# First modulation of a hybrid diffusion block: from split row products to raw fp32 weights as stationary operand

## The chip, the cores and the metric

One core of a Trainium2 chip. The metric is device time in microseconds of one execution; lower is better. The kernel is one layer of a diffusion backbone on 1024 latent tokens and 256 context tokens of width 1024, all in fp32.

## What is computed

The change touches the first few steps of the layer, the modulation vectors and the first RMSNorm:

```python
mod_l = (jax.nn.silu(c) @ w_mod[i] + b_mod[i])[:, None, :]
mod_c = jax.nn.silu(c_ctx) @ w_mod[i] + b_mod[i]
sh1, sc1, g1, sh2, sc2, g2 = jnp.split(mod_l, 6, axis=-1)
csh1, csc1, cg1, csh2, csc2, cg2 = jnp.split(mod_c, 6, axis=-1)
hl = modulate(rmsnorm(xl, norm1_w[i]), sh1, sc1)      # rmsnorm * (1 + scale) + shift
hc = modulate(rmsnorm(xc, norm1_w[i]), csh1, csc1)
...
xbc_l, dt_l, z_l, f_l, uv_l, gate_l = jnp.split(hl @ w_in, IN_SPLIT, axis=-1)
```

Everything after it (state space scan, Fourier mixing, gated MLPs, convolutional MLP, final norm) uses `hl` and `hc`, directly or through what is made of them.

## The kernel before

Tokens lie along the free dimension, channels on the partitions: `xT` holds the latent tokens as 8 tiles of 128 channels x 1024 tokens, `ctxT` the context. Large products run on TensorE in the reduced type fp32r, each operand split into a high and a low part (`split`, `wsplit`): ScalarE (ACT) copies the high part, VectorE (DVE) or GpSimd (POOL) subtracts to get the low part, and `mm3` adds three products, high x high, high x low and low x high. Small or delicate products run in plain fp32 with no split; the trace shows each of these as two TensorE records.

The start of the program, which the change touches, has these steps:

- **Squares (L194 to L204).** ACT squares the 8 tiles of `xT` as they land (L198, L201). DVE adds them into two accumulators `qx` (L202, six adds) and these into one (L203). `tok_sums` (L188) then sums over the partitions on TensorE: eight fp32 products with 128 columns of `qx` as stationary operand and one column of ones as moving operand, into `psx`.
- **Norm factor (`rstd_bcast`, L171).** DVE scales the sum (`rvx`, L173), POOL takes the power -0.5 (`rrx`, L175), DVE builds two diagonal tiles (`dgx`, L180), TensorE spreads them over the partitions with a matrix of ones (L183), ACT copies the result to `rbx`. The same for the context (`pssc`, `rrc`, `rbc`).
- **Modulation rows (`mod_rows(k)`, L234).** For each of 8 channel tiles k, two weight tiles `wm` (128 x 4 x 256) are split (ACT L239, POOL or DVE L240), and 16 products (L243) stream 256 weight columns past a 4-column stationary operand `csp`, the high and low parts of silu(c) and silu(c_ctx). The result is 4 rows of 256; DVE copies it to `mrow` (L246), and two fp32 products with the selector `sel` (L257) turn it into columns and add high and low.
- **Normalised tokens (L258 to L273).** DVE finishes `mods` (L258, L260), scales `xT` by it (L266), ACT adds the shift into the high part `hh` (L267), DVE makes the low part `hl` (L268); the same for the context (L271 to L273).
- **First products of the projection.** As tile k of `hh` and `hl` is there, TensorE adds its share to `psx` of weight tile `wx8` (L153, L155, L157), to the context's `psc`, and to the two halves of `psdl` (`dt_mm`, L356): per step k ten records with 512 columns and three with 256. When all 8 steps are in, the convolution on `psx` starts and the rest of the program follows.

The order of instructions on each engine is fixed when the program is built, by a scheduler that works on the dependencies; `tc.high_priority` moves a step ahead in it. Each engine then works strictly in its order. All transfers go out on SP's queue.

Of the kernel before, what the change touches and what calls it, by code (L numbers as in the profile page):

```python
# [8 lines left out]
F32 = mybir.dt.float32  # L9
F32R = mybir.dt.float32r  # L10
AF = mybir.ActivationFunctionType
ALU = mybir.AluOpType
AX = mybir.AxisListType

P = 128
D = 1024
KT = D // P
L = 1024
LC = 256
NH = 16  # L20
NCH = L // P
# [6 lines left out]
PRE, CRIT, CHAIN = 250, 200, 700  # L28
# [4 lines left out]
def hybrid_block_kernel(ctx: ExitStack, tc: tile.TileContext, a, dbg=None):  # L33
    nc = tc.nc
    V, S, G, PE, SY = nc.vector, nc.scalar, nc.gpsimd, nc.tensor, nc.sync

    def pool(name, bufs=1, **kw):
        return tc.alloc_tile_pool(name=name, bufs=bufs, **kw)

    const = pool("const")  # L40
# [11 lines left out]
    def ps_small(name, tag="c"):  # L52
        return pss.tile([P, 512], F32, tag=tag, name=name)
# [6 lines left out]
    def bc(ap, shape):  # L60
        return ap.broadcast_to(shape)
# [4 lines left out]
    s2 = pool("s2", bufs=2, side="right")  # L66
# [3 lines left out]
    ident, ones = cst[:, 0, :], cst[:, 1, :]  # L70
# [3 lines left out]
    wm0 = []  # L74
# [39 lines left out]
    sc_ = const.tile([P, KT, 2], F32, name="silc")  # L114
    S.activation(sc_, cvec, AF.Tanh, scale=0.5)
    V.scalar_tensor_tensor(sc_, sc_, 1.0, cvec, op0=ALU.add, op1=ALU.mult)
    V.tensor_scalar(sc_, sc_, 0.5, None, op0=ALU.mult)
    csp = const.tile([P, KT, 4], F32R, name="csp")
    S.activation(csp[:, :, 0:2], sc_, AF.Copy)
    V.tensor_tensor(csp[:, :, 2:4], sc_, csp.bitcast(F32)[:, :, 0:2], op=ALU.subtract)  # L120
    sel = const.tile([4, 2], F32, name="sel")
    V.tensor_tensor(sel, ident[0:4, 0:2], ident[0:4, 2:4], op=ALU.add)

    def late_consts():
        r = [load(sh, a[n], n) for sh, n in (([P, KT], "n2w"), ([P, KT], "nfw"), ([P, KT], "ssdd"), ([P, KT], "ssdn"),
                                             ([P, 44, 3], "fconvw"), ([P, 44], "fconvb"))]
        return r
# [31 lines left out]
    def f32(t):  # L159
        return t.bitcast(F32)  # L160
# [10 lines left out]
    def rstd_bcast(ss, n, dim, out, diag, tags, name, scale=1.0):  # L171
        v_ = const.tile([P, 16], F32, tag="rs_v", name="rv" + name, bufs=2)
        V.tensor_scalar(v_[:, 0:n], ss, scale / dim, EPS, op0=ALU.mult, op1=ALU.add)  # L173
        r_ = const.tile([P, 16], F32, tag="rs_r", name="rr" + name, bufs=2)
        G.tensor_tensor(r_[:, 0:n], v_[:, 0:n], expo[:, 0:n], op=ALU.pow)  # L175
        for i, tg in enumerate(tags):
            m = min(4, n - 4 * i)
            w_ = m * P
            dg = diag[:, 512 * i:512 * i + w_]
            V.tensor_tensor(dg.rearrange("p (n c) -> p n c", n=m), bc(ident.unsqueeze(1), [P, m, P]),  # L180
                            bc(r_[:, 4 * i:4 * i + m].unsqueeze(2), [P, m, P]), op=ALU.mult)
            ps = ps_small(f"rb{name}{i}", tg)
            last_op["PE"] = PE.matmul(ps[:, 0:w_], ones, dg, start=True, stop=True)  # L183
            if out is not None:
                S.activation(out[:, 512 * i:512 * i + w_], ps[:, 0:w_], AF.Copy)
        return ps[:, 0:w_]

    def tok_sums(ps, src, n, c0=0):  # L188
        for t in range(n):
            PE.matmul(ps[:, c0 + t:c0 + t + 1], src[:, t * P:(t + 1) * P], ones[:, 0:1], start=True, stop=True)  # L190


    psx = ps_small("psx", "c")
    qx = [tpool.tile([P, L], F32, tag=("tmp", "zz")[i], name=f"qx{i}", bufs=1) for i in range(2)]  # L194
    for k in range(KT):
        xk = xT[k // 4][:, k % 4, :]
        if k < 2:
            S.activation(qx[k], xk, AF.Square)  # L198
            continue
        q = s2.tile([P, L], F32, tag="CT", name=f"sqx{k}")  # L200
        S.activation(q, xk, AF.Square)  # L201
        V.tensor_tensor(qx[k % 2], qx[k % 2], q, op=ALU.add)  # L202
    V.tensor_tensor(qx[0], qx[0], qx[1], op=ALU.add)  # L203
    tok_sums(psx, qx[0], NCH)  # L204
    ssx = psx[:, 0:NCH]
    rbx = tpool.tile([P, L], F32, tag="tmp", name="rbx", bufs=1)
    dgx = tpool.tile([P, L], F32, tag="zz", name="dgx", bufs=1)
    with tc.high_priority(offset=CHAIN):
        rstd_bcast(ssx, NCH, float(D), rbx, dgx, ("y", "c2"), "x")

    hch = ctxp.tile([P, KT, LC], F32R, name="hch")
# [15 lines left out]
    rstd_bcast(ssc, 2, float(D), rbc, dgc, ("y",), "c")  # L227
    psmod = ps_small("psmod", "t")
    mods = const.tile([P, KT, 2, 2], F32, name="mods")
    crow = [p_[0:4, 256:512] for p_ in (psmod, ps_small("psrow", "c"))]  # L230
    mrt = s2.tile([4, 2, 256], F32, tag="CT", name="mrow")
    mrow = [mrt[:, i, :] for i in range(2)]

    def mod_rows(k):  # L234
        for i in range(2):
            wm = wm0[k][i]
            wh = s2.tile([P, 4, 256], F32R, tag="BT", name=f"wmh{k}{i}")
            wl = s2.tile([P, 4, 256], F32R, tag="Bt", name=f"wml{k}{i}")
            S.activation(wh, wm, AF.Copy)  # L239
            (G if i == 0 and k > 1 else V).tensor_tensor(wl, wm, f32(wh), op=ALU.subtract)  # L240
            for r in range(4):
                for q in range(2):
                    PE.matmul(crow[k % 2], csp[:, 4 * i + r, :], (wh, wl)[q][:, r, :], start=i + r + q == 0,  # L243
                              stop=i + r + q == 5)
        with tc.high_priority(offset=CHAIN):
            V.tensor_copy(mrow[k % 2], crow[k % 2])  # L246

    Hr = [dram.tile([P, L], F32, name=f"Hr{k}") for k in range(KT)]
    hh = [None] * KT
    hl = [None] * KT  # L250
    raws = []
    for k in range(KT):
        mod_rows(k)
        with tc.high_priority(offset=CHAIN):
            for s_ in range(2):
                o = 4 * k + 2 * s_
                PE.matmul(psmod[:, o:o + 2], mrow[k % 2][:, s_ * P:(s_ + 1) * P], sel, start=True, stop=True)  # L257
            V.tensor_tensor(mods[:, k], psmod[:, 4 * k:4 * k + 4].rearrange("p (s v) -> p s v", s=2),  # L258
                            bc(bmod[:, k:k + 9:8].unsqueeze(2), [P, 2, 2]), op=ALU.add)
            V.scalar_tensor_tensor(mods[:, k, 1], mods[:, k, 1], 1.0, bc(n1w[:, k:k + 1], [P, 2]),  # L260
                                   op0=ALU.add, op1=ALU.mult)
        shl, Al, shc, Ac = mods[:, k, 0, 0:1], mods[:, k, 1, 0:1], mods[:, k, 0, 1:2], mods[:, k, 1, 1:2]
        hh[k] = hpool.tile([P, L], F32R, tag="h", name=f"hh{k}")
        hl[k] = hpool.tile([P, L], F32R, tag="h", name=f"hl{k}")
        xk = xT[k // 4][:, k % 4, :]
        V.scalar_tensor_tensor(xk, xk, Al, rbx, op0=ALU.mult, op1=ALU.mult)  # L266
        last_op["hh"] = S.activation(hh[k], xk, AF.Identity, bias=shl)  # L267
        V.scalar_tensor_tensor(hl[k], xk, shl, f32(hh[k]), op0=ALU.add, op1=ALU.subtract)  # L268
        raws.append((k, xk, shl))
        ck = ctxT[k // 4][:, k % 4, :]  # L270
        V.scalar_tensor_tensor(ck, ck, Ac, rbc, op0=ALU.mult, op1=ALU.mult)  # L271
        S.activation(hch[:, k, :], ck, AF.Identity, bias=shc)
        last_op["h"] = V.scalar_tensor_tensor(hcl[:, k, :], ck, shc, f32(hch)[:, k, :],  # L273
                                              op0=ALU.add, op1=ALU.subtract)
# [317 lines left out]
    BT, Bt, CT = gi  # L592
# [115 lines left out]
    for g in range(4):  # L708
        psF = [ps_small(f"psF{g}{i}", ("c", "c2")[i]) for i in range(2)]
        for l_ in range(NCH):  # L710
            PE.matmul(psF[l_ // 4][:, (l_ % 4) * P:(l_ % 4 + 1) * P], fT[g][:, l_ * P:(l_ + 1) * P], tabc,
                      start=True, stop=True)
# [525 lines left out]
    def wpair(src, nm, raw=None):  # L1238
        if raw is None:
            raw = wx.tile([P, HB], F32, tag="rw", name=f"r{nm}", bufs=5)  # L1240
            SY.dma_start(raw.rearrange("p (k c) -> p k c", c=P), src)
        t = wpool.tile([P, 2, HB], F32R, tag="w", name=f"p{nm}")
        S.activation(t[:, 0, :], raw, AF.Copy)  # L1243
        G.tensor_tensor(t[:, 1, :], raw, f32(t)[:, 0, :], op=ALU.subtract)  # L1244
        v = t.rearrange("p q (k c) -> p q k c", c=P)
        return v[:, 0], v[:, 1]
# [23 lines left out]
    for d in PAIRS:  # L1270
        sg = tpool.tile([P, L], F32, tag="acc", name=f"sf{d}")
        SY.dma_start(sg, Sg[1][d])
        with tc.high_priority(offset=PRE):
# [5 lines left out]
            wh, wl = wpair(None, f"wfd{d}", we.rearrange("p a b c -> p (a b c)"))  # L1279
# [3 lines left out]
        for par, n in enumerate((NE, NO)):  # L1283
            o, q = [(pa[par][:, 0:n], slice(0, n))], [(pb[par][:, 0:n], slice(0, n))]
# [18 lines left out]
    for g in range(4):  # L1303
        t = tpool.tile([P, L], F32, tag=("tmp", "zz")[g % 2], name=f"gm{g}", bufs=1)
# [5 lines left out]
    for i, d in enumerate(PAIRS):  # L1310
# [9 lines left out]
        p_, th_, tl_ = (hpool, "h", "h") if d < 4 else (xp, "x", "x")  # L1320
# [186 lines left out]
    for ci, kc in enumerate(FF_CHUNKS[:-1]):  # L1507
# [3 lines left out]
        for i in range(0, len(seq), 2):  # L1511
            m = min(2, len(seq) - i)
            r = xp.tile([P, 2, HB], F32, tag="x", name=f"gr{ci}{i}")
            for q in range(m):
                p, k = seq[i + q]
                SY.dma_start(r[:, q, :], Gd[j0 // 2 + k][:, WHERE[p], :])
            p_, th_, tl_ = (xp, "x", "x") if i < 8 and ci < 3 else (hpool, "h", "h")
# [197 lines left out]
```

## Time and profile before

| | us |
|---|---|
| median of 3 runs (lowest, highest) | 1870.4 (1862.96, 1873.94) |
| the profiled execution, its own time | 1878.45 |
| its span in the profile | 1876.6 |
| TensorE (PE) busy in it | 1751.9 |
| VectorE (DVE) busy | 1347.3 |
| ScalarE (ACT) busy | 899.3 |
| GpSimd (POOL) busy | 808.3 |

The profiled execution lies 0.4% above the median; 1.85 us of it lie outside the span. All instants below are microseconds from the start of the span.

### The profile page before, as it was taken

What the parts mean: (1) busy time and instruction counts of PE and PEld (TensorE: products, weight loads), DVE (VectorE), ACT (ScalarE), POOL (GpSimd) and SP (SyncE); (2) the same over time, 40 slices, a digit from 0 to 9 for tenths busy, and PEclk for the clock granted to TensorE, in tenths of its full rate; (3) what the DMA queues carried; (4) which work ended last, traced back from release to release, by engine and by line L of the source; (5) the groups of instructions that cost most, each with busy time, mean ns of one, the idle gap of its engine ahead of it and who ended that gap; (6) DMA issues with size and microseconds to landing.
All of it is one profiled execution on the core that took longest, in us unless ns stands there. A gap on an engine that the chain in (4) does not pass through costs nothing. (4 is left out here: it accounts for less than half of the span.)

```text
span 1876.6 us, 23660 instructions
## 1 busy us (share of the span) xinstructions
PE 1751.9 (93%) x8172; PEld 1413.7 (75%) x8172; DVE 1347.3 (72%) x1855; ACT 899.3 (48%) x1605; POOL 808.3 (43%) x541
## 2 busy tenths in 40 slices
PE   4899998988999989999899999989999999899988
PEld 3688676776678868888688888868888888677767
DVE  6775668658873765558849535988878787977986
ACT  5544366665752344445434235545555455533433
POOL 3222254326531555444646745433333333554443
PEclk8899999999999989999998999999999999999998
DMA  9212374634563325665346364022332235653532
GB/s 337 90 60 67 102 202 139 188 111 143 156 227 123 123 74 196 230 223 181 118 141 207 129 230 135 29 90 102 117 108 96 96 108 172 231 168 107 169 91 90
DMA packets 147487, 267.70 MB, mean 143 GB/s; under 512 B 15772, under 2 KB 56604, under 8 KB 145960
## 3 DMA queue, kind: packets, MB, share of 16 engines
q1 hardware_dynamic: 147368, 266.20, 43.4%
q8 instruction: 64, 1.05, 0.2%
q14 instruction: 55, 0.45, 0.1%
HBM read 208.85 MB, written 57.29 MB: 142 GB/s over the span
## 5 line engine op out<-in xcount | busy, mean ns | idle before, releaser
L293 DVE SCALAR_TENSOR_TENSOR acc<-psx,convw,acc 128x1023 f32<-128x1023 f32 (+1 forms) x48 | 61.3, 1276 | 27.1 <-ACT acc L289 26.9
L568 DVE SCALAR_TENSOR_TENSOR rf<-rs,ncuml,rf 128x128 f32<-128x128 f32 x128 | 56.2, 487 | 29.5 <-ACT rf L567 21.2
L1244 POOL TENSOR_TENSOR pwo<-rwo,pwo 128x512 fp32r<-128x512 f32 x32 | 47.0, 1475 | 47.0 <-ACT pwo L1243 43.5
L861 POOL TENSOR_TENSOR w1up<-A11up,w1up 128x512 fp32r<-128x512 f32 x20 | 27.9, 1395 | 72.3 <-ACT w1up L860 72.3
L166 ACT ACTIVATE gh<-gr 128x1024 fp32r<-128x1024 f32 (+1 forms) x36 | 37.1, 1032 | 40.6 <-DMA gr<-Gd 37.8
L861 POOL TENSOR_TENSOR w7up<-S3up,w7up 128x512 fp32r<-128x512 f32 x18 | 23.7, 1317 | 74.5 <-ACT w7up L860 39.4
L567 ACT ACTIVATE rf<-rf,ncuml 128x128 f32<-128x128 f32 x128 | 40.8, 390 | 29.2 <-DMA rf<-Rd 27.1
L1531 DVE SCALAR_TENSOR_TENSOR xf<-Yd,g,xf 128x512 f32<-128x512 f32 x64 | 46.8, 742 | 10.0 <-PE Yd L871 10.0
L157 PE MATMUL pso<-mh,pwo 128*128 128x512 f32 x128 | 50.2, 392 | 0.0
L153 PE MATMUL pso<-mh,pwo 128*128 128x512 f32 x128 | 49.8, 390 | 0.0
L155 PE MATMUL pso<-ml,pwo 128*128 128x512 f32 x128 | 49.8, 389 | 0.0
L574 ACT ACTIVATE rs<-cbm,dtl 128x128 f32<-128x128 f32 x128 | 44.9, 390 | 7.9 <-DVE rf L568 7.7
L570 ACT ACTIVATE G<-cbm,dtl 128x128 f32<-128x128 f32 x128 | 40.6, 390 | 13.7 <-DVE cbm L556 9.3
L1446 ACT ACTIVATE aa<-aa 128x512 f32<-128x512 f32 x44 | 27.7, 629 | 36.6 <-DVE aa L1428 36.2
L529 POOL TENSOR_TENSOR st<-st,etl 128x512 f32<-128x512 f32 x24 | 32.1, 1339 | 27.4 <-DVE st L531 27.4
L167 DVE TENSOR_TENSOR gl<-gr,gh 128x1024 fp32r<-128x1024 f32 (+1 forms) x26 | 37.7, 1454 | 5.3 <-ACT gh L166 4.5
L861 POOL TENSOR_TENSOR w4up<-A22up,w4up 128x512 fp32r<-128x512 f32 x20 | 29.5, 1476 | 26.7 <-ACT w4up L860 25.2
L514 PEld LDWEIGHTS po<-CT,st 128*128 128x128 f32 x224 | 31.5, 205 | 11.0 <-DVE st L531 5.2
L1448 DVE TENSOR_TENSOR gt<-gt,aa 128x512 f32<-128x512 f32 x44 | 37.8, 862 | 2.3 <-ACT aa L1446 2.1
L581 PE MATMUL py<-rf,Xf 128*64 128x128 f32 x256 | 21.1, 287 | 18.9 <-DVE rf L576 12.8
L575 DVE TENSOR_TENSOR G<-G,rs 128x512 f32<-128x512 f32 x32 | 27.7, 865 | 14.6 <-ACT rs L574 14.5
L514 PE MATMUL po<-CT,st 128*128 128x128 f32 x224 | 34.5, 296 | 3.5 <-DVE st L531 3.4
(1330 smaller groups left out, 6603.1 us busy)
## 6 DMA issues: line engine op xcount, KB each, us to landing
gr<-Gd SPq DMA_DIRECT2D x70, 256.0 KB, 3.6
Gd<-gt SPq DMA_DIRECT2D x10, 1536.0 KB, 5.7
wm<-in_wmod_dram SPq DMA_DIRECT2D x16, 512.0 KB, 9.7
ro<-Rd SPq DMA_DIRECT2D x64, 128.0 KB, 3.9
rf<-Rd SPq DMA_DIRECT2D x32, 256.0 KB, 4.5
rs<-Rd SPq DMA_DIRECT2D x32, 256.0 KB, 3.7
ctanh<-in_wmod_dram SPq DMA_DIRECT2D x32, 256.0 KB, 4.4
crow<-in_wmod_dram SPq DMA_DIRECT2D x32, 256.0 KB, 4.4
```

What stands on the lines that cost most here:

```text
L153: PE.matmul(o, wh[:, k, :], xh[:, sl], start=st, stop=False)
L155: PE.matmul(o, wh[:, k, :], xl[:, sl], start=False, stop=False)
L157: last_op["mm"] = PE.matmul(o, wl[:, k, :], xh[:, sl], start=False, stop=sp)
L293: V.scalar_tensor_tensor(acc[:, lo:hi], ps[:, lo + o:hi + o], cw[:, t, j:j + 1], acc[:, lo:hi], op0=ALU.mult, op1=ALU.add)
L514: PE.matmul(po[:, i * P:(i + 1) * P], st[:, i * P:(i + 1) * P], CT[:, c * P:(c + 1) * P], start=True, stop=True)
L567: S.activation(E[:, h, :], E[:, h, :], AF.Identity, bias=ncum[:, c, f:f + 1])
L568: V.scalar_tensor_tensor(E[:, h, :], rs[:, h, :], ncum[:, c, 16 + f:17 + f], E[:, h, :], op0=ALU.add, op1=ALU.min)
L570: S.activation(Gm[:, h, :], cbm[:, 0, :], AF.Copy, scale=dtl[:, c, f:f + 1])
L574: S.activation(rs[:, h, :], cbm[:, 1, :], AF.Copy, scale=dtl[:, c, f:f + 1])
L861: (V if p in on_v else G).tensor_tensor(t[:, 1, :], ap, f32(t)[:, 0, :], op=ALU.subtract)
L1244: G.tensor_tensor(t[:, 1, :], raw, f32(t)[:, 0, :], op=ALU.subtract)
L1531: V.scalar_tensor_tensor(xv, src, g2[:, dd:dd + 1], xv, op0=ALU.mult, op1=ALU.add)
```

## The change

The squares of the last two channel tiles are no longer added by DVE: TensorE sums four tiles (`qx[0]`, `qx[1]`, and the squares of tiles 6 and 7) with 32 products into 32 columns of `psx`, and one DVE reduction adds the four. The weight tiles of the modulation are no longer split: 128 columns of a raw fp32 tile are the stationary operand and the two columns of silu(c), silu(c_ctx) the moving one, which gives the modulation as columns at once. `csp`, `sel`, `crow`, `mrow`, the splits, the row copies and the selector products go.

```diff
-    csp = const.tile([P, KT, 4], F32R, name="csp")
-    S.activation(csp[:, :, 0:2], sc_, AF.Copy)
-    V.tensor_tensor(csp[:, :, 2:4], sc_, csp.bitcast(F32)[:, :, 0:2], op=ALU.subtract)
-    sel = const.tile([4, 2], F32, name="sel")
-    V.tensor_tensor(sel, ident[0:4, 0:2], ident[0:4, 2:4], op=ALU.add)
...
-        q = s2.tile([P, L], F32, tag="CT", name=f"sqx{k}")
+        q = s2.tile([P, L], F32, tag="CT" if k < 6 else ("BT", "Bt")[k % 2], name=f"sqx{k}")
         S.activation(q, xk, AF.Square)
-        V.tensor_tensor(qx[k % 2], qx[k % 2], q, op=ALU.add)
-    V.tensor_tensor(qx[0], qx[0], qx[1], op=ALU.add)
-    tok_sums(psx, qx[0], NCH)
-    ssx = psx[:, 0:NCH]
+        if k < 6:
+            V.tensor_tensor(qx[k % 2], qx[k % 2], q, op=ALU.add)
+        else:
+            qx.append(q)
+    for i, q in enumerate(qx):
+        tok_sums(psx, q, NCH, NCH * i)
+    ssx = const.tile([P, NCH], F32, name="ssx")
...
+        V.tensor_reduce(ssx, psx[:, 0:NCH * len(qx)].rearrange("p (q t) -> p t q", t=NCH), axis=AX.X, op=ALU.add)
...
-    def mod_rows(k):
-        for i in range(2):
-            wm = wm0[k][i]
-            wh = s2.tile([P, 4, 256], F32R, tag="BT", name=f"wmh{k}{i}")
-            wl = s2.tile([P, 4, 256], F32R, tag="Bt", name=f"wml{k}{i}")
-            S.activation(wh, wm, AF.Copy)
-            (G if i == 0 and k > 1 else V).tensor_tensor(wl, wm, f32(wh), op=ALU.subtract)
-            for r in range(4):
-                for q in range(2):
-                    PE.matmul(crow[k % 2], csp[:, 4 * i + r, :], (wh, wl)[q][:, r, :], start=i + r + q == 0,
-                              stop=i + r + q == 5)
-        with tc.high_priority(offset=CHAIN):
-            V.tensor_copy(mrow[k % 2], crow[k % 2])
+    def mod_cols(k):
+        for s_ in range(2):
+            o = 4 * k + 2 * s_
+            for r in range(KT):
+                PE.matmul(psmod[:, o:o + 2], wm0[k][r // 4][:, r % 4, s_ * P:(s_ + 1) * P], sc_[:, r, :],
+                          start=r == 0, stop=r == KT - 1)
...
     for k in range(KT):
-        mod_rows(k)
+        mod_cols(k)
         with tc.high_priority(offset=CHAIN):
-            for s_ in range(2):
-                o = 4 * k + 2 * s_
-                PE.matmul(psmod[:, o:o + 2], mrow[k % 2][:, s_ * P:(s_ + 1) * P], sel, start=True, stop=True)
```

The order on TensorE at the start, before (`psx<-cst,qx` are the token sums, `wmh` and `wml` the split weight tiles of step 0, `pssc` the context's sums):

```order
L243 MATMUL psmod<-wmh_260,csp 4x256
L190 MATMUL psx<-cst,qx_175 128x1 x8
L243 MATMUL psmod<-wml_261,csp 4x256
...
L223 MATMUL pssc<-cst,qc_223 128x1 x4
L183 MATMUL rbx_213<-dgx,cst 128x512
L183 MATMUL rbx_217<-dgx,cst 128x512
L257 MATMUL psmod<-sel,mrow 128x2 x2
```

and of the change (`wm_111` and `wm_113` are the raw weight tiles of step 0, `silc` the silu columns):

```order
L184 MATMUL psx<-cst,qx_170 128x1 x8
L184 MATMUL psx<-cst,qx_171 128x1 x8
L184 MATMUL psx<-cst,sqx_186 128x1 x8
L184 MATMUL psx<-cst,sqx_188 128x1 x8
L233 MATMUL psmod<-silc,wm_111 128x2 x4
...
L221 MATMUL pssc<-cst,qc_241 128x1 x4
L233 MATMUL psmod<-silc,wm_111 128x2 x2
L177 MATMUL rbx_231<-dgx,cst 128x512
...
L177 MATMUL rbc_263<-dgc,cst 128x256
L233 MATMUL psmod<-silc,wm_121 128x2 x4
```

All 32 token sums now stand first, then step 0's products with those of the norm factor among them, then step 1's, before the first product of the projection. Later on TensorE, before (tail of step 3's projection products, then the rows of step 4):

```order
L155 MATMUL psx_597<-hl_364,wx8h 128x512 x2
L157 MATMUL psx_597<-hh_363,wx8l 128x512 x2
L356 MATMUL psdl_672<-hl_364,wdt 64x512
L155 MATMUL psc_646<-hcl,wx8h 128x256
L157 MATMUL psc_646<-hch,wx8l 128x256
L243 MATMUL psrow<-wmh_445,csp 4x256
L257 MATMUL psmod<-sel,mrow 128x2 x2
```

and of the change (the modulation of step 4, then the projection products of step 3):

```order
L233 MATMUL psmod<-silc,wm_137 128x2 x4
L233 MATMUL psmod<-silc,wm_139 128x2 x4
L233 MATMUL psmod<-silc,wm_137 128x2 x4
L233 MATMUL psmod<-silc,wm_139 128x2 x4
L147 MATMUL psx_525<-hh_372,wx8h 128x512 x2
L149 MATMUL psx_525<-hl_373,wx8h 128x512 x2
L151 MATMUL psx_525<-hh_372,wx8l 128x512 x2
L147 MATMUL psc_574<-hch,wx8h 128x256
...
L341 MATMUL psdl_599<-hh_372,wdt 64x512
```

From step 2 on the 16 modulation products of a step now stand together, between the projection products of the two steps before it; both halves of `psdl` stand in the step. On DVE one step before:

```order
L246 COPY mrow<-psrow 4x256
L240 TENSOR_TENSOR wml_421<-wm_139,wmh_420 128x1024
L258 TENSOR_TENSOR mods<-psmod,bmod 128x4
L268 SCALAR_TENSOR_TENSOR hl_364<-xT_97,mods,hh_363 128x1024
L260 SCALAR_TENSOR_TENSOR mods<-mods,n1w 128x2
L273 SCALAR_TENSOR_TENSOR hcl<-ctxT_115,mods,hch 128x256
```

and of the change:

```order
L243 TENSOR_TENSOR mods<-psmod,bmod 128x4
L245 SCALAR_TENSOR_TENSOR mods<-mods,n1w 128x2
L251 SCALAR_TENSOR_TENSOR xT_98<-xT_98,mods,rbx 128x1024
L256 SCALAR_TENSOR_TENSOR ctxT_116<-ctxT_116,mods,rbc 128x256
L253 SCALAR_TENSOR_TENSOR hl_399<-xT_98,mods,hh_398 128x1024
L258 SCALAR_TENSOR_TENSOR hcl<-ctxT_116,mods,hch 128x256
```

The step on DVE is now free of row copies and weight splits. On POOL the first split `wx8l` and that of `wdt` now stand ahead of `rrx`, behind which they stood; behind the start, the orders of all engines differ only by small exchanges up to the second scan.

## Rows read from the trace of the kernel before

**Rows 1.** The page: span and busy time

```profile
span 1876.6 us, 23660 instructions
PE 1751.9 (93%) x8172; PEld 1413.7 (75%) x8172; DVE 1347.3 (72%) x1855; ACT 899.3 (48%) x1605; POOL 808.3 (43%) x541
```

**Rows 2.** Windows: start, loop, and what follows; stretch, length, engines, clock, DMA

```profile
core 0: us, PE busy (x) PEld busy (x) DVE busy (x) ACT busy (x) POOL busy (x), PEclk, DMA share, GB/s
18.00:33.30 15.30, 12.85 (x53) 8.52 (x54) 12.62 (x16) 8.11 (x12) 7.14 (x4) 0.86 1.04 402
33.30:92.90 59.60, 49.30 (x244) 33.48 (x243) 47.88 (x62) 35.56 (x41) 20.03 (x7) 0.83 0.36 137
92.90:200.00 107.10, 102.56 (x601) 89.50 (x600) 74.28 (x122) 48.03 (x74) 27.07 (x11) 0.98 0.22 71
...
200.00:300.00 100.00, 87.53 (x395) 64.74 (x394) 65.75 (x98) 52.16 (x125) 41.23 (x27) 0.91 0.56 153
```

**Rows 3.** Groups of instructions by line, first 100 us

```profile
L240 POOL TENSOR_TENSOR wml<-wm,wmh 128x1024 fp32r<-128x1024 f32 x6 | 17.0, 2834 | 23.4 <-ACT wmh L239 23.4
L239 ACT ACTIVATE wmh<-wm 128x1024 fp32r<-128x1024 f32 x16 | 16.6, 1051 | 8.3 <-PE psrow L243 3.8 <-POOL wml L240 2.7 <-PE psmod L243 1.0
L240 DVE TENSOR_TENSOR wml<-wm,wmh 128x1024 fp32r<-128x1024 f32 x10 | 14.0, 1403 | 1.1 <-ACT wmh L239 1.1
```

**Rows 4.** DVE and POOL in order of time: adds, norm factor, first tokens

```profile
10.12 7.66 DVE L202 TENSOR_TENSOR qx<-qx,sqx 128x1024 f32<-128x1024 f32 x6 [6.51 <-ACT sqx L201]
...
23.40 2.07 POOL L175 TENSOR_TENSOR rrx<-rvx,expo 128x8 f32<-128x8 f32 x1 [22.98 <-DVE rvx L173]
25.43 2.35 POOL L139 TENSOR_TENSOR wx8l<-wx8r,wx8h 128x1024 fp32r<-128x1024 f32 x1
27.74 1.18 POOL L350 TENSOR_TENSOR wdt<-wdr,wdt 128x256 fp32r<-128x256 f32 x1
...
25.50 3.97 DVE L180 TENSOR_TENSOR dgx<-cst,rrx 128x512 f32<-128x512 f32 x2 [1.53 <-POOL rrx L175]
```

**Rows 5.** PE in order of time, 19 to 43 us: sums and rows at half clock

```profile
19.09 3.57 PE L190 MATMUL psx<-cst,qx 128*128 128x1 f32 x16 [0.59 <-DVE qx L203]
22.53 0.37 PE L243 MATMUL psmod<-wml,csp 128*4 128x256 f32 x1
...
28.39 3.21 PE L183 MATMUL rbx<-dgx,cst 128*128 128x512 f32 x4 [1.73 <-DVE dgx L180]
...
42.04 0.97 PE L153 MATMUL psx<-hh,wx8h 128*128 128x512 f32 x2
```

**Rows 6.** PE around 1122 us: the same kind of sums at full clock

```profile
1122.58 1.84 PE L190 MATMUL pnn<-cst,qn 128*128 128x1 f32 x16
1124.28 0.48 PE L153 MATMUL pso<-mh,pwo 128*128 128x512 f32 x1
```

**Rows 7.** PE: projection products at half clock, then at full, and the last one

```profile
80.26 1.05 PE L157 MATMUL psx<-hh,wx8l 128*128 128x512 f32 x2
81.11 0.63 PE L356 MATMUL psdl<-hl,wdt 128*64 128x512 f32 x1
...
53.07 0.63 PE L157 MATMUL psx<-hh,wx8l 128*128 128x512 f32 x2
53.53 0.39 PE L356 MATMUL psdl<-hl,wdt 128*64 128x512 f32 x1
...
92.77 0.28 PE L157 MATMUL psc<-hch,wx8l 128*128 128x256 f32 x1
```

**Rows 8.** Windows: the granted clock around two stretches of work

```profile
1838.30:1841.40 3.10, 3.10 (x28) 3.02 (x27) 0.75 (x1) 0.59 (x1) 0.00 (x0) 1.00 0.00 0
1841.70:1845.00 3.30, 3.30 (x9) 2.60 (x8) 1.52 (x3) 0.00 (x0) 1.02 (x1) 0.50 0.00 0
...
46.40:49.50 3.10, 3.10 (x9) 2.29 (x9) 3.10 (x5) 1.20 (x2) 0.00 (x0) 0.50 0.50 201
49.70:53.00 3.30, 3.30 (x24) 2.57 (x25) 2.29 (x6) 2.08 (x3) 0.06 (x1) 1.00 0.39 159
```

More of the change, by code (lines that the diff above doesn't have):

```diff
@@ L229, in hybrid_block_kernel @@
     mods = const.tile([P, KT, 2, 2], F32, name="mods")
-    crow = [p_[0:4, 256:512] for p_ in (psmod, ps_small("psrow", "c"))]
-    mrt = s2.tile([4, 2, 256], F32, tag="CT", name="mrow")
-    mrow = [mrt[:, i, :] for i in range(2)]
-    def mod_rows(k):
-        for i in range(2):
-            wm = wm0[k][i]
-            wh = s2.tile([P, 4, 256], F32R, tag="BT", name=f"wmh{k}{i}")
-            wl = s2.tile([P, 4, 256], F32R, tag="Bt", name=f"wml{k}{i}")
-            S.activation(wh, wm, AF.Copy)
-            (G if i == 0 and k > 1 else V).tensor_tensor(wl, wm, f32(wh), op=ALU.subtract)
-            for r in range(4):
-                for q in range(2):
-                    PE.matmul(crow[k % 2], csp[:, 4 * i + r, :], (wh, wl)[q][:, r, :], start=i + r + q == 0,
-                              stop=i + r + q == 5)
-        with tc.high_priority(offset=CHAIN):
-            V.tensor_copy(mrow[k % 2], crow[k % 2])
+    def mod_cols(k):
[4 more added lines that the diff above has]
+                          start=r == 0, stop=r == KT - 1)
     Hr = [dram.tile([P, L], F32, name=f"Hr{k}") for k in range(KT)]
```

## The prediction

> **What bounds the kernel now.** I read the page first, then the windows of the start, the groups of the changed lines, and TensorE's (PE's) instructions in order of time.
>
> The page says that PE is busy 93% of the span [rows 1]. That is a mean; what this change is worth is read in the first 93 us. The windows show three stretches [rows 2]: the start, up to 33.3 us; the loop over 8 channel tiles, up to 92.9 us; and what follows. In the loop PE is busy 49.3 us of 59.6, DVE 47.9, ACT 35.6, POOL 20.0: nothing is full, PE and DVE wait for each other, and the mean granted clock of PE is 0.83. In the next stretch PE is busy 102.6 of 107.1 us at 0.98. So a microsecond gained or lost at the end of the loop reaches the end of the program, unless a later stretch gives it back. The loop ends on PE with the last product of the context, 92.77 + 0.28, or 93.0 us [rows 7]: this is the mark that I price the change against.
>
> **What goes away.** ACT loses 16 copies of 1051 ns, 16.6 us; DVE 10 subtractions, 14.0 us, besides the eight row copies and three of the seven adds of squares; POOL 6 subtractions, 17.0 us [rows 3]. Of DVE's 47.9 us in the loop some 30 are left, under 4 us a step. On PE 128 row products of 256 columns go, and 16 selector products. A row product of 256 columns costs half of one of 512. Products of 512 start 0.425 us apart at the half clock (80.26 to 81.11, two of them) and 0.23 us apart at the full one (53.07 to 53.53) [rows 7]; so the rows cost 16 x 0.21 = 3.4 us a step at half clock and 1.85 us at full.
>
> **What comes.** Each step now has 16 fp32 products with 128 stationary columns and two moving ones. The nearest rows are the token sums, the same form with one moving column, two records a product. At half clock 16 records take 22.53 - 19.09 = 3.44 us, 0.215 us a record [rows 5]. At full clock 16 records push the next product from 1122.58 to 1124.28, 0.106 us a record [rows 6]. The cost halves with the clock and hardly any column moves: it is the loading of the stationary operand. The 32 records of a step cost 32 x 0.215 = 6.9 us at half clock and 3.4 us at full, about twice what the rows cost at the same clock. So PE, which the change was not short of in the loop, gets more work, and the three engines that get less were not full either.
>
> The Trainium skill ("TensorE: Matmul & The Clock Gate", LDWEIGHTS) prices a load at columns / 1.2 ns whatever the clock, 107 ns for 128 columns, and "FP8 and Floating Point Precision" (TensorE Precision Notes) counts four passes for true fp32. As an estimate from these two, a step would cost 64 x 107 ns = 6.8 us at either clock. The half-clock row agrees, the full-clock row (0.106 us where two passes would make 0.214) does not. By the skill's price the loop below would end at about 118 us, 25 us late.
>
> **The lead-in.** DVE's adds alternate between the two accumulators; the first is now complete after the third add, three times 7.66 / 6 = 1.28 us from 10.12, at 13.96 us [rows 4], and the second one add later. From there 32 sums, 64 records, stand first in PE's queue: 13.8 us at half clock, which the start has (the rows and sums up to 25 us run at it [rows 5]). They end at 27.7 us; before, they ended at 22.5. The reduction on DVE, one short instruction, is priced at the nearest small one, under 0.2 us, and hidden by step 0's products. Behind the sums stand step 0's products, 6.9 us; the context's sums, 8 records, 1.7 us; the norm factors, 3.2 us for `rbx` [rows 5] and a quarter of that, 0.8, for `rbc`; and step 1's products, 6.9 us. The sum is 27.7 + 19.5 = 47.2 us for the first projection product, which stood at 42.04 [rows 5]. The chain over POOL and DVE (splits 2.35 and 1.18, power 2.07, diagonal 3.97 [rows 4]) runs beside this and does not end later: the two splits are done while the sums run.
>
> **The loop.** PE then has 8 steps of projection products and 6 of modulation. A projection step is ten records of 512 columns and three of 256: 11.5 x 0.425 = 4.9 us at half clock, 11.5 x 0.23 = 2.65 us at full. Everything at half: 8 x 4.9 + 6 x 6.9 = 80.6 us. Everything at full: 8 x 2.65 + 6 x 3.4 = 41.6 us. Nothing else ends later: with DVE under 4 us a step, `hl` of a step is there before PE has done the modulation of the next.
>
> **Which clock.** This decides the case. Around 1838 us PE is busy without a gap for 3.1 us at clock 1.00, with 28 records, nearly all of them token sums,, and then the grant falls to 0.50 for the next stretch, 1841.7 to 1845 [rows 8]. The other way, a stretch of projection products at 0.50, 46.4 to 49.5, is followed by one at 1.00 [rows 8]. So work that only loads weights seems not to keep the clock, and projection products seem to win it back. In the changed loop the two kinds alternate. I take each kind to run half of its work at either level: (80.6 + 41.6) / 2 = 61.1 us. The loop would end at 47.2 + 61.1 = 108.3 us, **15.3 us later** than 93.0. The bounds are 47.2 + 80.6 = 127.8 us, 34.8 us later, and a loop all at full clock, worked out under the first rival.
>
> **The sum.** I carry 15 us through to the end. The profiled execution took 1878.45 us, which would become 1893.5; it lies 8 us over the median of 1870.4. Put on the median, the forecast is **1885.4 us**, 0.8% slower. About 0.5%, 9.4 us, can be told from no change here.
>
> **The rivals.**
>
> *A: loading keeps the clock full, and the change is faster.* The mechanism is that weight loads without a gap count as work like any other, from the lead-in on. For it: PE would no longer idle some 10 us in the loop [rows 2], and idling before a fall is seen too. Against it: the fall after 1841.4 with no idling [rows 8]. At full clock the loop takes 41.6 us; from the old start, 42.04, it ends at 83.6 us, 9.4 us early: 1861. From the lead-in at half clock, 47.2, it ends at 88.8, 4 us early. If DVE's four weight splits and the row copy that lie ahead of the first product (4 x 1.4 + 0.4 = 6.0 us) also shorten the start, it ends at 77.6, 15 us early: 1855. Where it decides: from 47.2 us the loop may take 45.8 us, so once a tenth of its work runs at half clock ((45.8 - 41.6) / 39 = 0.11) nothing is left to gain. The Trainium skill ("TensorE: Matmul & The Clock Gate", Part 1) tells it this way: the clock is throttled by default and sustained busy PE releases it; read as busy time, this speaks for A. The trace shows a busy PE losing its clock.
>
> *B: the projection products do not win the clock back.* Between two modulation stretches there are only 4.9 us of them. Then nearly all runs at half clock and the loop ends at 127.8 us: 1870.4 + 34.8 = 1905. Against it: the rise after 3.1 us of such products [rows 8].
>
> *C: the delay is taken up later.* From 200 to 300 us PE idles 12.5 us, at clock 0.91 [rows 2]; transfers or splits that are ready earlier by the delay could shorten these waits, and the small exchanges in the order could do it too. At most 12.5 of 15.3 come back: 1873, no change that can be told. Against it: before 200 us PE is full, and what it waits for later starts from products of its own.
>
> **How the numbers follow.** Chances: forecast 0.48, A 0.25, B 0.13, C 0.14. Faster by over 0.5% is what A gives when the start shortens too, three fifths of A: 0.15. Within 0.5% are the rest of A, 0.10, nearly all of C, 0.12 after its tail, and 0.02 of the forecast's: 0.24. Slower by over 0.5%: 0.61. The range, 1858 to 1903 us, takes in the forecast, most of A, C, and half of B; the forecast's own range is 1878 to 1896.
>
> **What the profile will show.** Right: about 256 records on the new modulation line, 0.21 us apart in stretches at 0.50; token sums at the start ending near 27.7 us; the last context product of the loop at 103 to 115 us; mean clock in the loop well under 0.83; DVE under 35 us busy there. A: records 0.11 us apart throughout and the loop over before 89 us. B: a clock near 0.5 from 30 to 125 us. C: the loop late as forecast, but marks after 300 us not. The forecast is wrong altogether if a product with two moving columns costs other than one with one column, or if `hl` comes late, which waits of PE for DVE in the loop would show.

## The result, and the profile after

The changed kernel took 1887.35 us (median of 4 runs, 1885.8 to 1890.96), the kernel before 1870.92 beside it (4 runs). The ratio is 1.0084, with a 95% interval of 1.0061 to 1.0107: **slower by 0.8%**, some 16 us. The forecast was 1885.4.

The page after, against [rows 1]: DVE, ACT and POOL each have less to do, PE has 30 us more.

```profile
span 1884.4 us, 23891 instructions
PE 1781.8 (95%) x8316; PEld 1455.3 (77%) x8316; DVE 1313.7 (70%) x1833; ACT 883.4 (47%) x1588; POOL 791.5 (42%) x535
```

PE in order of time, after, with columns as in [rows 5]: the sums, the last modulation products of the lead-in, three modulation steps of the loop with the projection product behind each, the last product of the context. The last row is the answer to [rows 6].

```profile
14.56 6.99 PE L184 MATMUL psx<-cst,qx 128*128 128x1 f32 x32 [14.56 <-DVE qx L197]
21.41 6.97 PE L184 MATMUL psx<-cst,sqx 128*128 128x1 f32 x32
28.23 4.41 PE L233 MATMUL psmod<-silc,wm 128*128 128x2 f32 x20
...
41.17 6.83 PE L233 MATMUL psmod<-silc,wm 128*128 128x2 f32 x32
47.86 1.20 PE L147 MATMUL psx<-hh,wx8h 128*128 128x512 f32 x2
...
51.93 4.78 PE L233 MATMUL psmod<-silc,wm 128*128 128x2 f32 x32
56.57 1.20 PE L147 MATMUL psx<-hh,wx8h 128*128 128x512 f32 x2
...
70.29 4.08 PE L233 MATMUL psmod<-silc,wm 128*128 128x2 f32 x32
74.23 0.86 PE L147 MATMUL psx<-hh,wx8h 128*128 128x512 f32 x2
...
87.60 3.97 PE L233 MATMUL psmod<-silc,wm 128*128 128x2 f32 x32
91.43 0.97 PE L147 MATMUL psx<-hh,wx8h 128*128 128x512 f32 x2
...
107.67 0.28 PE L151 MATMUL psc<-hch,wx8l 128*128 128x256 f32 x1
...
1138.17 1.84 PE L184 MATMUL pnn<-cst,qn 128*128 128x1 f32 x16
```

The sums end at 28.2, the loop starts at 47.86 instead of 42.04 [rows 5] and ends at 107.67 + 0.28, or 107.95, instead of 93.05 [rows 7]: 14.9 us late. A step's 32 modulation records take 47.86 - 41.17 = 6.7 us where the clock is at its lower level, 0.21 us a record. The same sums that stood at 1122.58 [rows 6] now stand at 1138.17, 15.6 us late.

The windows after: the whole loop, then a modulation stretch, a projection stretch and the next pair of them, then what follows.

```profile
core 0: us, PE busy (x) PEld busy (x) DVE busy (x) ACT busy (x) POOL busy (x), PEclk, DMA share, GB/s
47.80:108.00 60.20, 60.20 (x298) 51.51 (x299) 26.14 (x45) 20.52 (x23) 0.03 (x1) 0.72 0.17 69
52.00:56.50 4.50, 4.50 (x33) 4.50 (x32) 0.66 (x2) 1.15 (x1) 0.00 (x0) 0.74 0.28 117
56.60:61.30 4.70, 4.70 (x14) 3.59 (x15) 3.60 (x6) 1.83 (x3) 0.00 (x0) 0.53 0.01 3
61.40:65.20 3.80, 3.80 (x33) 3.80 (x32) 0.00 (x0) 0.77 (x1) 0.00 (x0) 0.90 0.33 138
65.30:70.20 4.90, 4.90 (x14) 3.70 (x14) 3.69 (x6) 2.07 (x3) 0.00 (x0) 0.50 0.00 0
108.00:200.00 92.00, 87.42 (x502) 75.61 (x501) 61.95 (x107) 40.04 (x63) 21.76 (x9) 0.98 0.20 65
```

In the loop PE is busy all the 60.2 us (49.3 of 59.6 before, [rows 2]) at a mean clock of 0.72 (0.83 before); it waits for no other engine there at all. DVE, which had 47.9 us, has 26.1. The four stretches show a regular cycle: the clock falls late in a modulation stretch (0.74, 0.90 over the whole of it), the projection products behind it pay for it (0.53, 0.50), and it comes back where they end (at 61.0 us) or just behind them (at 71.2). After the loop the clock is 0.98 on both sides.

The printed 0.72 is a little too high. The trace after holds no clock record ahead of 50.75 us, and the view counts such a stretch as full clock, though the records just before the loop are 0.21 us apart. From 50.75 us to the end of the loop the mean is 0.70. Other loop windows below that begin ahead of the first clock record read too high in the same way.

Two groups of instructions answer to [rows 3]. The copies and subtractions of the weights are gone; the modulation line has 256 records, and the first thing that DVE does with a step's result, an add of four elements, waits for PE.

```profile
L233 PEld LDWEIGHTS psmod<-silc,wm 128*128 128x128 f32 x256 | 40.8, 247 | 3.4 <-issue 2.1 <-DVE hl L253 0.4
L243 DVE TENSOR_TENSOR mods<-psmod,bmod 128x4 f32<-128x4 f32 x8 | 1.3, 161 | 31.8 <-PE psmod L233 31.8
```

The delay holds for most of the program. Here is one and the same product with the same two waits, before and after, late in the program:

```profile
1640.89 0.47 PE L869 MATMUL Yd<-gh,w6d 128*128 128x512 f32 x1 [0.94 <-DVE xf L1531]
...
1642.12 0.50 PE L871 MATMUL Yd<-gh,w6d 128*128 128x512 f32 x1 [0.53 <-POOL w6d L861]
```

```profile
1655.85 0.47 PE L854 MATMUL Yd<-gh,w6d 128*128 128x512 f32 x1 [0.94 <-DVE xf L1516]
...
1657.08 0.50 PE L856 MATMUL Yd<-gh,w6d 128*128 128x512 f32 x1 [0.53 <-POOL w6d L846]
```

It is 1655.85 - 1640.89 = 14.96 us late, as at 108 us. The spans of the two profiled executions differ by 1884.4 - 1876.6 = 7.8 us only: 7 us of the delay come back in the last 230 us, which the change does not touch. From this product to the end the mean clock is 0.95 before and 0.96 after. The profiled executions of the experiments tell whether this belongs to the kernels. From the same product to the end of the span, the twelve of this case take 228.1 to 236.0 us: before 235.7, after 228.6, and the shortest of all is the kernel with the modulation products issued twice, whose loop ends latest. So I take it to be a difference of the executions, not of the kernels. The profiled execution of before lies 7.5 us above its median, the one of after 1.2 us below its own, and the medians differ by the whole 16 us. What lengthens this stretch in one execution and not in another is open.

### The profile page after: what moved, and what is told of

The parts are those of the page before. It is cut to its first block, busy times and chain, and to the rows that moved or that the text cites. A ratio compares the mean times of both kernels' runs of the same rounds, so it can differ in the third digit from the quotient of the medians.

```text
span 1884.4 us, 23891 instructions
## 1 busy us (share of the span) xinstructions
PE 1781.8 (95%) x8316; PEld 1455.3 (77%) x8316; DVE 1313.7 (70%) x1833; ACT 883.4 (47%) x1588; POOL 791.5 (42%) x535
## 5 line engine op out<-in xcount | busy, mean ns | idle before, releaser
L552 ACT ACTIVATE rf<-rf,ncuml 128x128 f32<-128x128 f32 x128 | 40.8, 389 | 30.6 <-DMA rf<-Rd 30.6
L1431 ACT ACTIVATE aa<-aa 128x512 f32<-128x512 f32 x44 | 27.7, 629 | 36.8 <-DVE aa L1413 36.4
L233 PEld LDWEIGHTS psmod<-silc,wm 128*128 128x128 f32 x256 | 40.8, 247 | 3.4 <-issue 2.1
```

The lines of the kernel that those rows point to most:

```text
L233: PE.matmul(psmod[:, o:o + 2], wm0[k][r // 4][:, r % 4, s_ * P:(s_ + 1) * P], sc_[:, r, :], start=r == 0, stop=r == KT - 1)
L552: S.activation(E[:, h, :], E[:, h, :], AF.Identity, bias=ncum[:, c, f:f + 1])
```

## Experiments

Theory **L** is the one of the prediction: 128-column loads with hardly a moving column cost 0.106 us at the full clock and twice that at the half, they lose the clock, and PE, with no gaps left, pays for it in the loop. The loop runs from the first projection product to the last product of the context. The rivals go by letters in the expectations, S for one that puts the delay down to the sums and W for one that puts it down to PE's work as such. Differences in us are the ratio times the median of the kernel before beside it.

### The change's modulation with the sums of before

```diff
-        if k < 6:
-            V.tensor_tensor(qx[k % 2], qx[k % 2], q, op=ALU.add)
-        else:
-            qx.append(q)
-    for i, q in enumerate(qx):
-        tok_sums(psx, q, NCH, NCH * i)
+        V.tensor_tensor(qx[k % 2], qx[k % 2], q, op=ALU.add)
+    V.tensor_tensor(qx[0], qx[0], qx[1], op=ALU.add)
+    tok_sums(psx, qx[0], NCH)
```

> The change's modulation (raw fp32 weights as stationary operand) with the token sums of before (16 records). Theory L (the products that only load weights cost twice the rows and let the clock fall to half): the lead-in is 5 us shorter than in the change, the loop the same, so the loop ends near 103 us and the kernel is about 10 us slower than before. Rival S (the delay comes from the longer token sums at the start): the loop ends near 93 us and the kernel is as fast as before.

Measured: 1.0046 [1.0025, 1.0066], 8.6 us slower. Its loop, PE in order of time and the window:

```profile
23.10 3.55 PE L184 MATMUL psx<-cst,qx 128*128 128x1 f32 x16
...
47.00 1.20 PE L147 MATMUL psx<-hh,wx8h 128*128 128x512 f32 x2
...
103.17 0.28 PE L151 MATMUL psc<-hch,wx8l 128*128 128x256 f32 x1
```

```profile
47.00:103.30 56.30, 56.30 (x266) 47.31 (x267) 22.48 (x39) 17.64 (x20) 0.00 (x0) 0.73 0.18 74
```

The loop ends at 103.45, 10.4 us late, without one of the added sums. S falls as the main cause. What the sums add to it can be read too. This loop has 266 records on PE, the change's has 298. The 48 added records of the sums take 10.3 us of PE at the half clock ahead of the loop; here PE does modulation there instead, 96 records before its first projection product against 64 in the changed kernel. So the added sums push one step's 32 records into the loop, and its end goes from 103.45 to 107.95.

### The change's sums with the row products of before

The edit is the other half: the kernel before, with the lines of the change from the squares to the reduction.

> The change's token sums (64 records) with the modulation rows of before. Theory L: the sums end 5 us later than before, 27.7 against 22.5 us, and the loop behind them shifts by about that, so 5 us slower than before, hard to tell from none. Rival S: all of the change's delay, 15 us.

Measured: 0.9986 [0.9974, 0.9997]. A miss: nothing is lost, and the interval lies just under 1. The sums do end some 5 us later, and so does what stands behind them, but the loop starts 2.5 us late and ends no later than the 93.05 of before:

```profile
20.40 6.97 PE L190 MATMUL psx<-cst,sqx 128*128 128x1 f32 x32
...
34.05 3.78 PE L183 MATMUL rbx<-dgx,cst 128*128 128x512 f32 x4 [1.73 <-DVE dgx L180]
...
44.56 1.12 PE L153 MATMUL psx<-hh,wx8h 128*128 128x512 f32 x2 [0.25 <-ACT hh L271]
...
92.50 0.28 PE L157 MATMUL psc<-hch,wx8l 128*128 128x256 f32 x1
```

```profile
44.50:92.80 48.30, 43.84 (x225) 29.63 (x226) 38.30 (x59) 31.38 (x37) 11.88 (x5) 0.89 0.26 98
```

In this loop PE is busy 43.8 of 48.3 us, at clock 0.89. With the splits of before, PE has gaps to take a delay up in; with the change's loads it has none. So the two halves of the change do not add up: the delay of the sums is free beside the old modulation and costs 4.5 us of the loop beside the new one. This loop is 48.2 us long, 2.8 us less than that of before, 51.0, though it has the rows of one step more in it. PE waits 4.5 us in it and 8.4 in that of before; what shortens the waits is not settled.

### The operands exchanged

The same fp32 products on the same raw weights, but with the two columns stationary and the weights moving; a row copy and two small transposing products a step come with it.

```diff
-        for s_ in range(2):
-            o = 4 * k + 2 * s_
-            for r in range(KT):
-                PE.matmul(psmod[:, o:o + 2], wm0[k][r // 4][:, r % 4, s_ * P:(s_ + 1) * P], sc_[:, r, :],
-                          start=r == 0, stop=r == KT - 1)
+        for r in range(KT):
+            PE.matmul(crow[k % 2], sc_[:, r, :], wm0[k][r // 4][:, r % 4, :], start=r == 0, stop=r == KT - 1)
+        with tc.high_priority(offset=CHAIN):
+            V.tensor_copy(mrow[k % 2], crow[k % 2])
+            for s_ in range(2):
+                o = 4 * k + 2 * s_
+                PE.matmul(psmod[:, o:o + 2], mrow[k % 2][:, s_ * P:(s_ + 1) * P], ident[0:2, 0:2], start=True, stop=True)
```

> The change with the operands exchanged: the two silu columns are the stationary operand and 256 columns of the raw fp32 weight tile stream past it, 8 fp32 products a step, still no splits; the result rows are copied by DVE and turned into columns by two small products. By the cycles of the records this is as much TensorE work a step as the change (16 records of 512 columns against 32 loads of twice 128). Theory L: streaming keeps the clock full, the loop takes some 45 us instead of 60 and ends at 88 to 95 us, so the kernel is 13 to 20 us faster than the change and about as fast as before. Rival W (only the amount of TensorE work counts, not its kind): as late as the change, 108 us, 15 us slower than before, or later for the copies.

Measured, with the change's sums: 1.0002 [0.998, 1.0024]. All of the loss is gone. The end of the lead-in and one step's modulation on PE, and the windows of the loop and of that step:

```profile
36.31 3.18 PE L235 MATMUL psrow<-wm,silc 128*2 128x256 f32 x14
39.42 0.70 PE L177 MATMUL rbc<-dgc,cst 128*128 128x256 f32 x2
...
40.57 0.73 PE L147 MATMUL psx<-hh,wx8h 128*128 128x512 f32 x2
...
62.37 3.62 PE L235 MATMUL psrow<-wm,silc 128*2 128x256 f32 x16
65.92 0.73 PE L147 MATMUL psx<-hh,wx8h 128*128 128x512 f32 x2
```

```profile
40.60:92.90 52.30, 49.71 (x230) 28.16 (x230) 28.54 (x55) 21.76 (x26) 0.00 (x0) 0.97 0.27 95
...
62.40:66.00 3.60, 3.60 (x18) 1.33 (x16) 2.07 (x4) 2.09 (x2) 0.00 (x0) 1.00 0.42 173
```

A step takes 65.92 - 62.37 = 3.55 us at the full clock; the change's 32 loads would take 32 x 0.106 = 3.4. PE has no less to do for the modulation, and is busy 95% of the loop. Yet the clock of the loop is 0.97 instead of 0.72, and the loop ends at 93.05 instead of 107.95. So W falls: lead-in and loop together, the same PE work costs 15 us less as streamed columns than as loads. This is the run that bears L out most directly.

The expectation put the whole gain into the loop, 45 us instead of 60. The loop takes 52.5 us, and the other half of the gain, 7.3 us, lies ahead of it: the streamed products hold the full clock in the lead-in already (the 14 records from 36.31 to 39.42 are 0.222 us apart, as in the step at 1.00), and the first projection product stands at 40.57 instead of 47.86.

### Exchanged, with the sums of before

The edits of the first and the third experiment together: fp32 throughout, no splits.

> The exchanged operands of the run before this one, with the token sums of before. Theory L: the lead-in is 5 us shorter too, the loop ends at 83 to 90 us, 3 to 10 us faster than before. Rival W: as the run with the change's modulation alone, some 10 us slower than before.

Measured: 0.9956 [0.9938, 0.9974], 8.2 us faster; the loop runs from 42.31 to 86.3 us at clock 0.96. As expected, and the fastest of the versions that keep the low parts.

### One pass

```diff
+    S.activation(csp, sc_, AF.Copy)
...
+            S.activation(wh[i], wm0[k][i], AF.Copy)
...
-                PE.matmul(psmod[:, o:o + 2], wm0[k][r // 4][:, r % 4, s_ * P:(s_ + 1) * P], sc_[:, r, :],
+                PE.matmul(psmod[:, o:o + 2], wh[r // 4][:, r % 4, s_ * P:(s_ + 1) * P], csp[:, r, :],
```

> The change, but the modulation takes only the high part of the weights and of silu (fp32r, one pass instead of four; ACT copies the high part, the low parts are left out, so the modulation is coarser). Still 128 stationary columns and two moving ones, 16 products a step, but a quarter of the loading. Theory L: a step's modulation costs under 1.8 us instead of 3.4 to 6.9, the projection products make up most of TensorE's time and the clock stays mostly full; the loop ends at 80 to 90 us, the kernel is 3 to 13 us faster than before. Rival N (it is the number of instructions, or the two-column form, that costs): little better than the change, loop end above 100 us.

Measured: 0.9899 [0.9872, 0.9926], 18.9 us faster than before (16.3 by the medians), which is more than expected; the loop ends at 77.4, earlier than expected. PE in order of time, with the loads in the lead-in, two pairs of products at the start of the loop and the loads of one step in it, and the loop's window:

```profile
27.14 3.55 PE L240 MATMUL psmod<-csp,wmh 128*128 128x2 f32 x16
30.55 1.84 PE L221 MATMUL pssc<-cst,qc 128*128 128x1 f32 x8
...
45.20 1.05 PE L149 MATMUL psx<-hl,wx8h 128*128 128x512 f32 x2
46.05 1.05 PE L151 MATMUL psx<-hh,wx8l 128*128 128x512 f32 x2
...
53.34 1.84 PE L240 MATMUL psmod<-csp,wmh 128*128 128x2 f32 x16
55.04 0.48 PE L149 MATMUL psx<-hl,wx8h 128*128 128x512 f32 x1
```

```profile
43.30:77.40 34.10, 32.80 (x186) 26.66 (x187) 24.71 (x44) 28.39 (x34) 0.00 (x0) 1.00 0.33 127
```

A record takes (30.55 - 27.14) / 16 = 0.213 us in the lead-in and (55.04 - 53.34) / 16 = 0.106 in the loop: just what each of the two records of an fp32 product takes. The expectation had a quarter of the loading where half is left: a step takes 1.70 us in the loop, against 3.4 at the same clock, and 3.4 in the lead-in.

The printed clock of 1.00 does not hold for the first 4 us of the loop: the first clock record stands at 47.13 us, and ahead of it two products of 512 columns take 46.05 - 45.20 = 0.85 us, the price of the half clock. From there on the loop, with half as many loads, keeps the full clock. N falls as to the price: the loop ends 30.6 us earlier than after, and the medians lie 32.6 us apart (1887.35 to 1854.74).

As to the clock, this edit halves the records on PE together with the loads, so it cannot tell the two apart. A stretch late in the changed kernel can:

```profile
1862.00:1872.00 10.00, 9.94 (x84) 9.63 (x82) 6.33 (x16) 4.66 (x14) 2.98 (x5) 1.00 0.24 93
```

PE has 84 records in these 10 us, nearly as close together as in the modulation stretch of the loop (33 in 3.8 us), and 82 loads of 128 columns. But 57 of these loads belong to products with 256 moving columns, and the clock stays at 1.00. So it is neither the number of records nor the loads as such that lose the clock, but loads with hardly a column streamed behind them.

### The modulation products issued twice

```diff
+        for s_ in range(2):
+            o = 64 + 4 * k + 2 * s_
+            for r in range(KT):
+                PE.matmul(psmod[:, o:o + 2], wm0[k][r // 4][:, r % 4, s_ * P:(s_ + 1) * P], sc_[:, r, :],
+                          start=r == 0, stop=r == KT - 1)
```

> The change with every modulation product issued a second time into unused columns of the same bank: 256 more records. Theory L: each step's loading doubles and the clock is at half for more of the loop, so the 256 records cost 0.15 to 0.21 us each, 40 to 55 us, and the loop ends at 148 to 163 us. Rival F (loading runs at full clock once it runs long enough): 0.106 us each, 27 us, loop end near 135 us.

One execution was measured, 1940.48 us. The loop's window:

```profile
61.20:162.00 100.80, 100.80 (x489) 92.03 (x490) 26.16 (x45) 20.30 (x23) 0.00 (x0) 0.63 0.09 37
```

The last context product ends at 162.2 us, 54.2 later than after, for 256 more records: 0.21 us each, as much as if every one of them ran at the half clock, with the mean clock at 0.63. L's span was right; F falls.

### Two attempts to use more projection products against the loss

If projection products win the clock back, more of them between the loads should help. The 48 projection records of the next tile, which the order puts behind the loop, were moved into it:

```diff
+    with tc.high_priority(offset=110):
+        psb10 = xbc_mm(10)[0]
...
-    with tc.issue_after(last_op["mm"].ins):
-        psb10 = xbc_mm(10)[0]
```

> The change, with the projection products of the next weight tile (48 records of 512 columns, which run right behind the loop in the change) moved into the loop, six a step: the same work, in another order. The mark is the first product of the tile after that, 119.6 us in the change. Theory L (column work wins the clock back, loading alone loses it): more column work between two loading stretches, so more of the loop at full clock; the mark comes at 111 to 118 us, 2 to 9 us earlier than in the change. Rival T (the clock goes by busy time or by chance): the mark stays within 1 us of 119.6, or later where more of these products run at half clock.

Measured: 1.0084 [1.0056, 1.0113], no gain over the change. By its mark the expectation missed: 121.82 us, later than the 119.57 of the change. The two windows are the loop with the moved products, and the hole behind it; the row is PE's first product of the next part. The last window is the same work after the change.

```profile
47.60:110.80 63.20, 63.20 (x344) 54.33 (x345) 26.14 (x45) 20.07 (x23) 1.50 (x1) 0.86 0.17 70
110.80:122.00 11.20, 1.52 (x11) 0.86 (x10) 10.20 (x13) 5.71 (x8) 3.24 (x2) 0.74 0.26 90
```

```profile
121.82 1.19 PE L147 MATMUL psx<-hh,wx0h 128*128 128x512 f32 x2 [7.03 <-DVE acc L278]
```

```profile
47.80:119.50 71.70, 71.70 (x353) 60.79 (x354) 37.03 (x61) 25.39 (x30) 2.49 (x2) 0.76 0.17 65
```

The same work (loop and moved products) runs to 119.5 us after the change, at clock 0.76; here it is done at 110.8, at 0.86. So T falls by the clock, though not by its mark: some of the clock was won back, and 8.8 us with it. But the products that used to fill PE while DVE does the convolution are now gone from there: PE waits 7 us for the accumulator, with both of the large accumulation buffers taken until the convolution is through, and the next part starts at 121.82 instead of 119.57. The gain turned into a wait that the expectation had not seen.

The same edit on the exchanged version with the old sums:

> Exchanged operands, token sums of before, and the next tile's projection products moved into the loop. The mark, 98.0 us with the exchanged operands alone, comes at 92 to 98 us if these products fill waits of TensorE in the loop, and the kernel is 8 to 14 us faster than before; it stays at 98 if TensorE has no waits left there or if they delay the step's own products.

Measured: 1.0036 [1.0017, 1.0056], slower than without the edit (0.9956). The same wait, 6.8 us here, stands ahead of that product, which comes at 104.08 us, later than either side of the expectation had it. The loop of the exchanged version was at 0.96 already, so there was hardly any clock to win back. A miss, by the same cause.

### Two versions with the high parts alone and the old sums

One pass with the weights stationary:

> Modulation from the high parts alone as stationary operand (the low parts are left out), with the token sums of before. If the start sets the loop's end here, the loop ends 4 to 6 us before the 77.4 us of the same modulation with the change's sums; if waits for VectorE set it, as in the run with the change's sums alone, it ends within 1 us of it.

Measured: 0.9896 [0.9874, 0.9918]; loop end 74.1, 3.3 us before that of one pass with the change's sums, and the total the same within the intervals. And one pass with the operands exchanged:

> The exchanged operands with the high parts alone (the low parts are left out): 8 records of 256 streamed columns a step in place of 16 loads of 128 columns, with two selector products and the row copy; token sums of before. By the records at full clock this is 0.9 us a step plus about 0.4 for the selector against 1.7 us for the loads, so at most 3 us better than the run before this one; if the row copy and the selector lengthen the wait of the step's tokens, a few us worse.

Measured: 0.9871 [0.9854, 0.9888], the lowest ratio of all, though its interval overlaps that of the run before it; loop end 74.3. With only 16 loads a step, or 8 products of streamed columns, the two forms end their loops within 0.2 us of each other, and in both the clock is 1.00 from 46 us to the end of the loop: the form matters where there are enough loads to lose the clock, and no longer here.

The end of the loop against the total, for all kernels with an interval but the two with moved products (the sums near 1100 us are those of [rows 6]):

| kernel | loop ends, us | sums near 1100 us at | ratio to before |
|---|---|---|---|
| before | 93.05 | 1122.6 | 1 |
| after | 107.95 | 1138.2 | 1.0084 |
| its modulation alone | 103.45 | 1129.2 | 1.0046 |
| its sums alone | 92.8 | 1121.1 | 0.9986 |
| exchanged | 93.05 | 1117.7 | 1.0002 |
| exchanged, old sums | 86.3 | 1110.4 | 0.9956 |
| one pass | 77.4 | 1102.1 | 0.9899 |
| one pass, old sums | 74.1 | 1104.1 | 0.9896 |
| one pass, exchanged, old sums | 74.3 | 1104.4 | 0.9871 |

What the loop gains or loses arrives at the end, give or take some 5 us that the long stages between take or give by themselves: the exchanged version shows that with a loop end equal to before and sums 4.9 us earlier. Differences under 5 us in the total are not explained by the loop.

## Why the prediction was right

The direction and the size came out, 1885.4 against 1887.35 us, and most terms with it.

- **What goes away is worth nothing.** Borne out: DVE fell from 47.9 to 26.1 us in the loop (forecast under 35), and its add waits 31.8 us for PE in eight steps. PE is the only engine that sets the pace.
- **The price of a record**, read off token sums with one moving column: 0.215 and 0.106 us. The records with two moving columns cost the same (6.85 us for 32 sums at 14.56, 6.7 for 32 modulation records at 41.17). Twice the records cost 0.21 us each again.
- **The lead-in.** Sums to end at 27.7, first projection product at 47.2: 28.2 and 47.86. They began 0.6 us later than worked out, and that is the whole difference.
- **The loop.** 61.1 us forecast, 60.1 measured; end 108.3 against 107.95. The least founded step was that each kind of work runs half at either level. Solving 41.6 + 39 w = 60.1 gives w = 0.47, but neither kind of work ran so. The six modulation steps take 4.64, 3.89, 3.94, 4.01, 3.83 and 4.13 us, 24.4 together, where 20.4 would be all full and 41.4 all half: they run mostly at the full clock and lose it. The other 35.7 us are projection products, where 21.2 would be all full and 39.2 all half: they run mostly at the half clock and pay. The size came out because the two errors cancel, and that was luck: the guess stood on windows with a fall and a rise, and could as well have been 0.3 or 0.7, which is 7 to 9 us either way. That the loads lose the clock and the products win it back was right.
- **The Trainium skill's price.** By the Trainium skill ("TensorE: Matmul & The Clock Gate", LDWEIGHTS), whose one price names no clock level, and with the four passes of the prediction, the loop would have ended at about 118. It ended at 107.95, so the row from the trace was the right price. The trace shows 32 loads a step (256 in eight steps), not 64, and in the one-pass run, with one load a product, a record takes 0.106 us at the full clock and 0.213 at the half. So the price of 107 ns fits a load at the full clock, and the agreement with the half-clock row came from counting twice the loads at half their price.
- **Rival A**, loads keep the clock: fell on the clock of 0.72 in a loop where PE is never idle. By the Trainium skill ("TensorE: Matmul & The Clock Gate", Part 1), read as busy time, PE should have kept it; here busy is not enough, and the exchanged version, no busier, keeps 0.97.
- **Rival B**, products never win it back: fell on the same stretches; a clock of 0.50 throughout would have ended the loop at 127.8.
- **Rival C**, the delay is taken up later: fell. From 200 to 300 us PE still waits, 9.7 of 100 us, but the delay behind it is no smaller: 15.6 us near 1122 us and 14.96 at 1655.
- **What the prediction did not see.** It carried the sums' delay as a term that adds to the loop. It does so only because PE has no gaps in the new loop; beside the old modulation the same delay costs nothing. And the mechanism is another than a late start: the loop starts 0.9 us later than with the old sums, but with one step of modulation more to do.

## What to carry to other kernels

Before making the large operand stationary to save splits and transposes, count the records that load 128 columns to stream one or two, and price them from a row of the trace at both clock levels. Then look at what stands behind them: a stretch that is nearly all loads, with hardly a column moving, can take the clock from the work that follows, and exchanging the operands, at the same PE time, kept it here. Freeing engines that PE does not wait for long buys little, and a delay that costs nothing while PE has gaps costs in full once the gaps are filled.

## What was not expected of the hardware

- Products that load 128 columns and stream two lose the clock although PE is busy without a gap (0.72 in the loop, 0.63 with twice as many), while fp32 products that stream 256 columns over a 2-column operand, 3.55 against 3.4 us a step, leave it at 0.97. Loads as closely spaced, with 256 moving columns behind most of them, left it at 1.00 (1862 to 1872 us).
- A record of a one-pass fp32r product with 128 stationary columns took 0.213 us at the half clock and 0.106 at the full, the same as each of the two records of an fp32 product: leaving the low parts out saved a factor of two, where the expectation had four.
- Of reading the profile: the window view prints a clock of 1.00 for stretches of the start for which the trace holds no clock record, such as the lead-in of the one-pass kernel, whose records are spaced 0.213 us, and the first microseconds of several loops. There the spacing of like records tells the clock, not the column.
